# The mixer stage of a hybrid backbone layer in a fixed order of pieces per block, with the projection weights of the mixer in the tiles of the old activations

## The chip, the cores and the metric

One Trainium2 chip, one core of it. The metric is device time of one execution in microseconds (us), smaller is better. Engines are named as in the profile: PE (TensorE, matmuls), DVE (VectorE), ACT (ScalarE), POOL (GpSimd), SP (SyncE, which here only issues DMAs). One DMA queue is fed by SP, another by POOL.

## What is computed

One layer on 1024 tokens of width 1024, with 256 context tokens ahead of them, all in fp32. Cut to what matters here:

```python
u_x = rms_norm(x, norm1_w) * (1 + sc1) + sh1
pr_x = _prep(u_x, w_in, conv_w, conv_b, ...)   # projections; q and k of the mLSTM go through a 3x3 depthwise conv + SiLU
x_hg_f, x_hg_b = HGRN2 scans, forward and backward;  x_ml_f, x_ml_b = mLSTM scans, forward and backward
hg = head_rms_norm(x_hg_f + x_hg_b) * silu(pr['hg_g'])
ml = head_layer_norm(x_ml_f + x_ml_b) * sigmoid(pr['ml_o'])
x  = x + g1 * (concat([hg, ml]) @ w_out)                      # the mixer
v  = rms_norm(x, norm2_w) * (1 + sc2) + sh2
aff = softmax(v @ router_w)                                   # 16 experts
gate, idx = top_k(aff.T, 128)                                 # each expert chooses 128 tokens
x  = x + g2 * scatter_add(gate * swiglu_e(v[idx]))            # 16 experts, 3 weights of 1024 x 1024 each
out = rms_norm(x, final_norm_w)
```

## The kernel before, in words

The 1024 tokens are 8 blocks of 128. Products in fp32 are made of three matmuls of halves: an operand is split into a rounded part (`uh`, `wh`, `mh`: "hi") and what is left (`ul`, `wl`, `ml`: "lo"), and hi\*hi, hi\*lo and lo\*hi are summed.

The program runs in stages: context, modulation and the first projections (0 to about 205 us of the span); HGRN2 (to 465); the output gates, the convs and the backward states of the mLSTM (to about 690, the tuple `ORD` sets the order of these pieces); the **mixer stage** (to 916); the choice of the tokens (to 952); the experts (to the end). `uh` and `ul`, the split activations, are two tiles of 32 KB a partition that live until the last gate piece "o144" has run. After that `upool.close()` gives their room to the pool `mpb`, which holds the split of `w_out` (`woh`, `wol`, eight tiles each, L1107 to L1113).

In the mixer stage a loop over blocks `cc` (L1128) calls, in this order: `mixer(cc)` (48 matmuls of 128x512, in two halves of 24, L1027; the residual is added on DVE, L1028; stored to d_acc on POOL's queue, L1029); `scores(cc+3)` (loads `qk`, L935, and then `MB`, L936, the broadcast of the running maxima, 1024 pieces of 512 B; four matmuls L939; eight biased copies on ACT, L943; a minimum with the causal mask on DVE, L944; an add on POOL, L946; two Exp, L945 and L947; products on DVE); `mixed(cc+1)` (loads `kin` and `go`; four scalings on ACT, L1005; products on DVE or POOL; 8 transposes L1012; split into `mh` and `ml`); `outputs(cc+2)` (loads `sb`; updates the forward state; for each head four matmuls L975/L976 into a bank, then absolute value, maximum L978, reciprocal and two scaled copies that empty the bank) with `normed` (statistics and scaling); and for the block before, `router` (sum of squares, reciprocal root, v = x r A + B as one DVE operation L1052 and one POOL add L1053, stored on POOL's queue) and `logits`/`affinity` (8 transposes L1038, 8 matmuls L1042, softmax). So three blocks are in work at once, and a scheduler interleaves these calls on each engine by its own estimates. Behind block 5 the first four token blocks are sorted (16 rounds of maximum and replace, L760/L762, and merges), and behind block 6 two more; the last two behind block 7.

Around it, weights of the experts are fetched ahead into whatever buffers are free ("raws", L892), and two operands `qkx` and `MB` have two buffers each: `MB` of block c+2 can only be loaded when the `outputs` of block c has read its own. [...]

The conv (L820 to L830, eight times) computes nine taps: one by ACT into the sum, two by ACT with a POOL add each (L825), six by DVE (L827).

## Time and profile before

| | |
|---|---|
| median of 3 runs | 1564.99 us (1562.31 to 1569.66) |
| the profiled execution | 1563.71 us, its span 1561.6 us |
| PE busy | 1443.4 us (92%) |
| DVE busy | 1227.9 us (79%) |
| ACT busy | 873.6 us (56%) |
| POOL busy | 213.7 us (14%) |
| stores of the mixer's blocks 0, 4 and 7 to d_acc are issued at | 746.7, 854.1 and 916.3 us |

The profiled execution is 1.3 us under the median, and 2.1 us of it lie outside the span. PE is the engine with most work, and its idle time and the clock that it is granted say what a stage could save; idle time of the others costs nothing by itself. The profile's rows are times from the start of the span.

### The profile page before, as it was taken

What the parts mean: (1) busy time and instruction counts of PE and PEld (TensorE: products, weight loads), DVE (VectorE), ACT (ScalarE), POOL (GpSimd) and SP (SyncE); (2) the same over time, 40 slices, a digit from 0 to 9 for tenths busy, and PEclk for the clock granted to TensorE, in tenths of its full rate; (3) what the DMA queues carried; (4) which work ended last, traced back from release to release, by engine and by line L of the source; (5) the groups of instructions that cost most, each with busy time, mean ns of one, the idle gap of its engine ahead of it and who ended that gap; (6) DMA issues with size and microseconds to landing.
All of it is one profiled execution on the core that took longest, in us unless ns stands there. A gap on an engine that the chain in (4) does not pass through costs nothing.

```text
span 1561.6 us, 23094 instructions
## 1 busy us (share of the span) xinstructions
PE 1443.4 (92%) x8113; PEld 1207.2 (77%) x8113; DVE 1227.9 (79%) x2148; ACT 873.6 (56%) x1478; POOL 213.7 (14%) x165
## 2 busy tenths in 40 slices
...
PEclk9999999999999999988999977999999999999998
...
GB/s 253 263 136 31 109 54 35 75 82 15 122 102 142 82 149 138 118 175 219 200 140 120 155 329 226 369 390 370 384 391 383 388 389 383 382 385 356 343 148 108
DMA packets 181199, 337.29 MB, mean 216 GB/s; under 512 B 13560, under 2 KB 108348, under 8 KB 181084
## 3 DMA queue, kind: packets, MB, share of 16 engines
...
q8 instruction: 64, 1.05, 0.3%
q14 instruction: 51, 0.42, 0.1%
HBM read 303.38 MB, written 32.39 MB: 215 GB/s over the span
## 4 chain that ended last, share of the span: by engine, by line
PE 67%; DVE 12%; DMA 8%; issue 6%; ACT 4%; POOL 3%; ACTq 0%; SPq 0%; POOLq 0%; DVEq 0%
PE mm L1293 21%; PE mm L278 12%; PE hg L1293 11%; PE mm L286 8%; PE hg L350 3%; DMA MB<-d_nm 3%; PE ms L1278 2%; PE hg L215 2%; DMA d_go<-gsg 1%; PE ms L382 1%; DVE cacc L827 1%; DVE ac L297 1%; POOL MB L946 1%; PE hg L1383 1%; POOL wor L1073 1%
## 5 line engine op out<-in xcount | busy, mean ns | idle before, releaser
L286 PE MATMUL mm<-whi,uh 128*128 128x256 f32 (+1 forms) x512 | 145.8, 285 | 1.7 <-DVE utmp L198 0.9
L286 PE MATMUL mm<-wlo,uh 128*128 128x256 f32 (+1 forms) x512 | 145.1, 283 | 0.0
L286 PE MATMUL mm<-whi,ul 128*128 128x256 f32 (+1 forms) x512 | 144.7, 283 | 0.0
L253 DVE TENSOR_TENSOR wlo<-wraw,whi 128x512 fp32r<-128x512 f32 x96 | 65.5, 696 | 51.0 <-ACT whi L252 50.6
L286 PEld LDWEIGHTS mm<-whi,uh 128*128 128x128 f32 x512 | 96.6, 189 | 4.0 <-DVE utmp L198 1.1
L286 PEld LDWEIGHTS mm<-whi,ul 128*128 128x128 f32 x512 | 96.8, 189 | 0.0
L286 PEld LDWEIGHTS mm<-wlo,uh 128*128 128x128 f32 x512 | 96.4, 188 | 0.2
L1293 PE MATMUL mm<-qkx,xT 128*128 128x512 f32 x256 | 83.8, 408 | 0.7 <-ACT xT L1279 0.3
L1293 PE MATMUL mm<-E,xT 128*128 128x512 f32 x256 | 80.9, 397 | 0.4 <-ACT E L922 0.4
L1293 PE MATMUL mm<-MB,xT 128*128 128x512 f32 x256 | 80.3, 395 | 0.0
L252 ACT CAST whi<-wraw 128x512 fp32r<-128x512 f32 x96 | 58.3, 620 | 38.7 <-PE mm L278 24.8
L827 DVE SCALAR_TENSOR_TENSOR cacc<-pad,cols,cacc 128x1024 f32<-128x1024 f32 x48 | 65.3, 1360 | 17.9 <-POOL cacc L825 17.2
L344 ACT COPY hgc<-hgK 128x512 f32<-128x512 f32 x56 | 35.5, 634 | 78.1 <-DVE hgK L363 38.6
L350 PE MATMUL hg<-hgQ,hgc 128*128 128x128 f32 x448 | 65.9, 291 | 1.0 <-DVE hgQ L366 1.0
L350 PEld LDWEIGHTS hg<-hgQ,hgc 128*128 128x128 f32 x448 | 57.8, 191 | 10.8 <-issue 6.7
L278 PE MATMUL mm<-uh,whi 128*128 128x512 f32 x192 | 63.4, 405 | 0.0
L278 PE MATMUL mm<-ul,whi 128*128 128x512 f32 x192 | 63.3, 403 | 0.0
L1308 POOL DMA_INDIRECT vt<-d_v,idx x16 | 16.7, 1044 | 328.7 <-PE ms L1278 252.3
L297 DVE SCALAR_TENSOR_TENSOR ac<-wraw,csil,ac 128x256 f32<-128x256 f32 x112 | 58.2, 520 | 4.4 <-DMA wraw<-in_ada_w_dram 2.5
L278 PE MATMUL mm<-uh,wlo 128*128 128x512 f32 x192 | 61.5, 399 | 0.0
L1293 PEld LDWEIGHTS mm<-E,xT 128*128 128x128 f32 x256 | 47.5, 187 | 13.8 <-ACT E L922 2.2
L825 POOL TENSOR_TENSOR cacc<-cacc,cone 128x1024 f32<-128x1024 f32 x16 | 40.2, 2512 | 124.7 <-ACT cone L824 124.1
...
## 6 DMA issues: line engine op xcount, KB each, us to landing
...
```

Source lines behind the costliest of these rows:

```text
L215: T.matmul(pm[0:2, :256], csil[:, k, :], adas[i, k // 4][:, k % 4, :, :], start=(k == 0), stop=(k == 7))
L252: S.copy(hi[:, :, cs], src)
L253: V.tensor_sub(lo[:, :, cs], src, hi[:, :, cs])
L278: T.matmul(o, l, r[:, k, i * n:(i + 1) * n], start=(k == 0 and q == 0), stop=(k == 7 and q == 2))
L286: T.matmul(o, l[:, k, ts], r, start=(k == 0 and q == 0), stop=(k == 7 and q == 2))
L297: V.scalar_tensor_tensor(ac, a2[:, k % 4, :], csil[:, k, 0:1], ac, op0=OP.mult, op1=OP.add)
L344: S.copy(view(kc, 0, [[h, 2], [2 * h, 256 // h], [1, h]]), view(K, 0, [[512 + h, 2], [2 * h, 256 // h], [1, h]]))
L350: T.matmul(pb[:, cc, :], kc[:, cc * P:(cc + 1) * P], view(Q, cc * P, pat), start=True, stop=True)
L825: G.tensor_add(acc, acc, one)
L827: V.scalar_tensor_tensor(acc, tap(t), tapw(t, r), acc, op0=OP.mult, op1=OP.add)
L1278: T.transpose(pt[:, k, :], view(src, 4 * q + k, [[8, P]]), ident)
L1293: T.matmul(o, l[:, k, :], r[:, 512 * j:512 * j + 512], start=(k == 0 and p_ == 0), stop=(k == 7 and p_ == 2))
```

## The change

- `uh` and `ul` become sixteen tiles of two k-slices by 512 columns each (the pool `up` stays open, `at` finds a slice). The splits of `w_out` take over those tiles one by one (`split_wo`): the first four (k 0 to 3, tiles `uh0x`, `ul0x`) are split before the last gate piece "o144", the other four behind it.
- The conv's tap 1 goes from DVE to ACT with a third POOL add.
- The causal mask is now 0 or -1e30 and is added instead of a minimum taken: by DVE for blocks 0 to 2, by POOL for the others (`s_min`).
- The scaling of `hg` by its norm is one broadcast multiply (`m_hg`), on DVE for blocks 0 and 1 and on POOL for the others; it was four ACT operations.
- v = x r A + B is now one ACT multiply and a POOL multiply and add (`r_v`); the DVE operation L1052 is gone. The stores of d_acc and d_v go from POOL's queue to SP's.
- `MB` is loaded ahead of `qk` in `s_load`.
- The functions are cut into pieces, and the loop over blocks calls them in a fixed order under `tc.manual_schedule()`: each engine runs them as written.
- The first sort, 16 rounds, runs in single rounds that are strewn over blocks 4 to 6 (`rounds`); the second, of two token blocks, runs on 128 partitions by 64 values in 8 rounds (before: 64 by 128 in 16), its pairs of lists are merged by `lists`.
- The loop's first weights are still split early by the scheduler; `A2b`, `B2b` and `g1b` join the raw buffers as operands.

The core of the diff:

```diff
-    uh = up.tile([P, 8, 1024], F32R, name="uh")
-    ul = up.tile([P, 8, 1024], F32R, name="ul")
+
+    uh, ul = ([[up.tile([P, 2, 512], F32R, name=f"{n}{hf}{j}", tag=f"{n}{hf}{j}", bufs=1) for j in range(4)] for hf in range(2)] for n in ("uh", "ul"))
+
+    def at(u, k, a, b):
+
+        return u[a // 512][k // 2][:, k % 2, a % 512:(b - 1) % 512 + 1] if isinstance(u, list) else u[:, k, a:b]
...
-    V.tensor_scalar(cmask[:, 0, :], dd, 0.5, 1e30, op0=OP.add, op1=OP.mult)
-    V.tensor_scalar(cmask[:, 1, :], dd, -1.0, 0.5, op0=OP.mult, op1=OP.add)
-    V.tensor_scalar(cmask[:, 1, :], cmask[:, 1, :], 1e30, None, op0=OP.mult)
+    V.tensor_scalar(cmask[:, 0, :], dd, 0.0, -1e30, op0=OP.is_lt, op1=OP.mult)
+    V.tensor_scalar(cmask[:, 1, :], dd, 0.0, -1e30, op0=OP.is_gt, op1=OP.mult)
...
-        for t in (3, 5):
+        for t in (3, 5, 1):
             one = cvp.tile([P, 16, 64], F32, name="cone", tag="cone", bufs=2)
             S.mul(one, tap(t), tapw(t, r))
             G.tensor_add(acc, acc, one)
-        for t in (0, 1, 2, 6, 7, 8):
+        for t in (0, 2, 6, 7, 8):
...
+    st = {}
+
+    def s_load(cc):
+        qk, MB = st["qk", cc], st["MB", cc] = tl("qkx", [8, P], 2), tl("MB", [8, P], 2)
+        load(MB, bass.AP(tensor=d_nm.tensor, offset=d_nm.offset + cc * P, ap=[[0, P], [1024, 8], [1, P]]))
         load(qk, d_qk[cc])
...
+    def s_min(cc, eng=V):
+        E = st["E", cc]
+        for d in range(2):
+            eng.tensor_tensor(E[:, d], E[:, d], cmask[:, d, :].unsqueeze(1).to_broadcast([P, 4, P]), op=OP.add)
...
+    def m_hg(cc, eng):
+        hg, go = st["hg", cc], st["go", cc]
+        mix = st["mix", cc] = tb("mix", [8, P], 1)
+        eng.tensor_mul(hg, hg, hgr[:, cc, :].unsqueeze(2).to_broadcast([P, 4, P]))
+        eng.tensor_mul(mix[:, 0:4, :], hg, go[:, 0:4, :])
+
+    def m_ml(cc):
+        V.scalar_tensor_tensor(st["mix", cc][:, 4:8, :], st["go", cc][:, 4:8, :], 1.0, st["h", cc], op0=OP.add, op1=OP.mult)
...
+    def x_store(cc):
+        load(d_acc[cc * P:(cc + 1) * P], st["xm", cc])
...
+    def r_v(cc):
+
+        vt = st["vt", cc]
+        S.mul(vt, st["xm", cc], st["r2", cc])
+        G.tensor_mul(vt, vt, A2b)
         G.tensor_add(vt, vt, B2b)
-        kept["v"] = store(d_v[row], vt)
-        if dbg and "xm" in dbg:
-            nc.sync.dma_start(dbg["xm"][row], xm)
-            nc.sync.dma_start(dbg["v"][row], vt)
-        return r2
-
-    def affinity(cc, r2, pl):
+
+    def v_store(cc):
+        load(d_v[cc * P:(cc + 1) * P], st["vt", cc])
...
+    def split_wo(ks):
+
+        for k in ks:
+            for l, n in ((woh, "uh"), (wol, "ul")):
+                l.append(up.tile([P, 1024], F32R, name=f"{n}{k // 4}{k % 4}", tag=f"{n}{k // 4}{k % 4}", bufs=1))
+            S.mul(woh[k], wors[k], onw[:, k:k + 1])
+            V.scalar_tensor_tensor(wol[k], wors[k], onw[:, k:k + 1], woh[k], op0=OP.mult, op1=OP.subtract)
+            if k + 3 < 8:
+                load_wo(k + 3)
...
-           "o004", "k3", "u4", "o044", "k2", "u3", "k1", "u2", "o104", "M", "u1", "S0", "S1", "O0", "L0", "o144")
+           "o004", "k3", "u4", "o044", "k2", "u3", "k1", "u2", "o104", "M", "u1", "S0", "S1", "O0", "W", "o144")
...
+    x_load(0)
+    m_load(0)
+    m_load(1)
+    m_hg(0, V)
+    m_ml(0)
+    m_T(0)
+    split_wo(range(4, 8))
...
+    for f in (o_load, o_state, o_step, o_num, n_stat):
+        f(1)
+    for f in (s_load, s_mm, s_kT, s_sum, s_min, s_exp):
+        f(2)
+    o_load(2)
...
+    def sort_steps(dst, src, n, w=P):
+
+        buf = srw[len(sorts)]
+        sorts.append(dst)
+        for r in range(w // 8):
+            e8 = dst[:n, 8 * r:8 * r + 8]
+            V.max(e8, src[:n])
+            if r < w // 8 - 1:
+                V.match_replace(buf[:n, :w], e8, src[:n], -1.0)
+            src = buf[:, :w]
+            yield
...
+    with tc.manual_schedule():
+        for cc in range(8):
+            a, b, c, p = cc + 1, cc + 2, cc + 3, cc - 1
+            if c < 8:
+                s_load(c)
+                o_load(c)
+            if b < 8:
+                m_load(b)
+            if cc:
+                x_store(p)
+            mixer(cc, 0, range(4))
+            if cc:
+                l_T(p)
+            if a < 8:
+                n_norm(a)
+                m_ml(a)
+            if cc:
+                r_v(p)
+                v_store(p)
+            mixer(cc, 0, range(4, 8))
+            x_add(cc, 0)
+            if b < 8:
+                s_mul(b)
+            rounds(3)
+            if c < 8:
+                s_mm(c)
+                s_sum(c)
+                s_min(c, G)
+            mixer(cc, 1, range(3))
+            if c < 8:
+                s_kT(c)
+            if cc == 7:
+                l_mm(p)
+                a_exp(p)
+                best = merge(srt[:, 0, :], (64, 32), tmp)
+                a_div(p)
+            mixer(cc, 1, range(3, 5))
+            if a < 8:
+                m_T(a)
+            if b < 8:
+                m_hg(b, G)
+            rounds(3)
+            if 0 < cc < 7:
+                l_mm(p)
+                a_exp(p)
+                a_div(p)
+            if b < 8:
+                o_state(b)
+                o_step(b)
+            if c < 8:
+                s_exp(c)
+            mixer(cc, 1, range(5, 8))
+            if a < 8:
+                x_load(a)
+            if b < 8:
+                o_num(b)
+            x_add(cc, 1)
+            r_sq(cc)
+            if b < 8:
+                n_stat(b)
+            r_rs(cc)
+            if cc in (1, 3, 5):
+                old(cc // 2)
+                raw_load(1)
+            if cc == 4:
+                pt = bank("ms")
+                T.transpose(pt[:, :P], aff[:, 0].rearrange("p s e -> p (s e)"), ident)
+                S.copy(affS[:, 0, :], pt[:, :P])
+                sorting.append(sort_steps(srt[:, 0, :], affS[:, 0, :], P))
+            if cc in (5, 6):
+                rounds(2)
+            if cc == 6:
+                pt = affinities(0, 2)
+                for h in range(2):
+                    S.copy(srt[64 * h:64 * h + 64, 1, 64:P], pt[0:64, 64 * h:64 * h + 64])
+                sorting.append(sort_steps(srt[:, 1, 0:64], srt[:, 1, 64:P], P, 64))
+                r_ = lambda n, sh: tl(n, sh, 2, F32R)
+                sl = [part(r_("qkx", [8, P])) if i % 3 == 0 else part(r_("MB", [8, P])) if i % 3 == 1 else
+                      r_("E", [2, 4, P]).rearrange("p a b c -> p (a b c)") for i in range(6)]
+                sl += [flat3(mlp.tile([P, 2, 4, 129], F32R, name="v3", tag="v3", bufs=1)),
+                       flat3(const.tile([P, 2, 4, 129], F32R, name="mlc", tag="mlc", bufs=1))]
+                pairs.extend((sl[2 * i], sl[2 * i + 1]) for i in range(4))
+                early = []
+        x_store(7)
+        l_T(7)
+        rounds(8)
+        l_mm(7)
+        a_exp(7)
+        b2 = lists(srt[:, 1, :], tmp[0])
+        a_div(7)
+    b2 = merge(b2, (32,), [tmp[2]])
+    best = top(32, best[:32], b2[:32], tmp[0])
...
+    early += [split_w() for _ in range(4)]
```

**First place: SP's queue at the entry of the mixer stage.** The names: `go` is the gate of `mixed`/`m_load` (L1002 before, L1044 after), `wor` with `in_w_out_dram` a row block of `w_out` (L1072 before, L1136 after; with `in_exp_w_gate_dram` it is a raw weight of an expert, L894), `xm` the residual (L1021, L1067). Before:

```order
L1002 DMA go_6919<-d_go_58 128x1024
L1115 DMA xT_6974<-in_router_w_dram 128x128
L1117 DMA mods_6976<-d_g_64 128x2x8
L1072 DMA wor_6945<-in_w_out_dram 128x1024
L1072 DMA wor_6950<-in_w_out_dram 128x1024
L1021 DMA xm_7094<-in_x_dram 128x1024
L1072 DMA wor_6955<-in_w_out_dram 128x1024
L936 DMA MB_7150<-d_nm_63 128x8x128
```

And now:

```order
L938 DMA MB_7085<-d_nm_63 128x8x128
L1136 DMA wor_6823<-in_w_out_dram 128x1024
L984 DMA sb_7117<-d_sb_61 128x516
L1136 DMA wor_6830<-in_w_out_dram 128x1024
L1136 DMA wor_6837<-in_w_out_dram 128x1024
L1136 DMA wor_6990<-in_w_out_dram 128x1024
L894 DMA wor_7012<-in_exp_w_gate_dram 128x1024
L1067 DMA xm_6958<-in_x_dram 128x1024
L1044 DMA go_6961<-d_go_58 128x1024
```

The first `go`, which the first transposes of the mixer need, stood ahead of all `wor` loads but the first three; it now stands behind all eight of them and behind the first raw weight, whose buffer is a `wor` buffer.

**Second place: SP's queue in one block of the loop.** Block 3 before (some of it is for neighbouring blocks):

```order
L935 DMA qkx_8041<-d_qk_57 128x1024
L1001 DMA kin_8259<-d_hg_59 128x512
L936 DMA MB_7812<-d_nm_63 128x8x128
L1021 DMA xm_7756<-in_x_dram 128x1024
L959 DMA sb_8093<-d_sb_61 128x516
L1002 DMA go_8260<-d_go_58 128x1024
```

and block 3 now:

```order
L938 DMA MB_7784<-d_nm_63 128x8x128
L939 DMA qkx_7783<-d_qk_57 128x1024
L984 DMA sb_7787<-d_sb_61 128x516
L1043 DMA kin_7789<-d_hg_59 128x512
L1044 DMA go_7790<-d_go_58 128x1024
L1084 DMA d_acc_66<-xm_7490 128x1024
L1117 DMA d_v_65<-vt_7764 128x1024
L1067 DMA xm_7944<-in_x_dram 128x1024
```

`MB` was behind `qk` (the `qk` of its own block is some rows further up still), and is now ahead of it; the two stores have come in from POOL's queue.

**Third place: PE in one block, around the matmuls of the scores** (L939 before, L946 now; L1027 and L1077 are the mixer, L480/L482 and L1012/L1061 transposes). Before:

```order
L1027 MATMUL mm<-wl_6915,mh 128x512
L1027 MATMUL mm<-wh_6914,ml 128x512
L939 MATMUL hg<-qkx 128x128 x4
L480 MATMUL ms<-ident,qkx 128x128 x4
L1012 MATMUL ms<-ident,mix 128x128 x4
L496 MATMUL mm<-v_4837,mkt 128x129 x4
```

And now:

```order
L1077 MATMUL mm<-ul_7002,mh 128x512
L1077 MATMUL mm<-uh_7001,ml 128x512
L946 MATMUL hg<-qkx 128x128 x4
L1077 MATMUL mm<-uh_6812,mh 128x512
L1077 MATMUL mm<-ul_6813,mh 128x512
L1077 MATMUL mm<-uh_6812,ml 128x512
L1077 MATMUL mm<-uh_6819,mh 128x512
L1077 MATMUL mm<-ul_6820,mh 128x512
```

The scores' matmuls stood behind all 48 matmuls of the mixer's block; they now stand behind the first 24 of them, and the other 24 behind them.

## Rows read from the trace of the kernel before

**Rows 1.** The page's first row and the row of part 2 that gives the clock granted to PE in 40 equal slices of the span (tenths of full speed).
```profile
span 1561.6 us, 23094 instructions
PEclk9999999999999999988999977999999999999998
```
**Rows 2.** Five stretches: from and to, length, then for PE, PEld, DVE, ACT and POOL the busy time and in brackets the instructions, PE's mean granted clock, DMA share, GB/s.
```profile
722.00:747.00 25.00, 20.34 (x78) 15.40 (x78) 23.78 (x36) 15.72 (x32) 13.98 (x8) 0.78 0.77 278
747.00:771.00 24.00, 18.92 (x110) 15.83 (x109) 17.05 (x45) 14.25 (x42) 8.83 (x7) 0.99 0.54 186
825.50:854.00 28.50, 23.33 (x137) 20.65 (x138) 15.94 (x44) 14.40 (x40) 8.85 (x7) 0.94 0.50 131
854.00:916.30 62.30, 58.69 (x316) 49.97 (x317) 49.00 (x193) 21.75 (x56) 17.01 (x16) 0.92 0.52 177
952.00:1540.00 588.00, 582.71 (x2714) 468.50 (x2714) 551.93 (x603) 452.33 (x542) 45.80 (x36) 1.00 0.94 346
```
**Rows 3.** POOL's timeline: the issues of three of the eight stores of the residual (start, duration, in brackets the idle time before).
```profile
746.72 0.79 POOL L1029 DMA_DIRECT2D d_acc<-xm  x1 [2.06 <-DVE xm L1028]
...
854.07 0.60 POOL L1029 DMA_DIRECT2D d_acc<-xm  x1 [3.31 <-DVE xm L1028]
...
916.30 0.54 POOL L1029 DMA_DIRECT2D d_acc<-xm  x1 [10.27 <-DVE tkr L760]
```
**Rows 4.** What ACT waited for from 716 to 922: total us, times, longest.
```profile
ACT E L943 <- DMA MB<-d_nm: 17.0, 5, 5.7
```
**Rows 5.** PE's timeline at full clock (a duration includes the pipeline; the pitch is the distance of two starts).
```profile
784.17 0.39 PE L1027 MATMUL mm<-wl,mh 128*128 128x512 f32 x1
784.40 0.39 PE L1027 MATMUL mm<-wh,ml 128*128 128x512 f32 x1
...
790.75 1.06 PE L939 MATMUL hg<-qkx 128*128 128x128 f32 x8
791.65 0.60 PE L480 MATMUL ms<-ident,qkx 128*128 128x128 f32 x4
```
**Rows 6.** SP's timeline: the issues of three of the loads of `MB`, and of the one behind the second.
```profile
778.31 0.43 SPq L936 DMA_DIRECT2D MB<-d_nm  x1
...
805.75 0.37 SPq L936 DMA_DIRECT2D MB<-d_nm  x1
...
834.25 0.43 SPq L936 DMA_DIRECT2D MB<-d_nm  x1
```
**Rows 7.** ACT's timeline: the first operation on each of these three `MB`, in brackets how long ACT had waited for it.
```profile
790.25 2.45 ACT L943 ACTIVATE E<-MB,gT 128x128 f32<-128x128 f32 x8 [5.65 <-DMA MB<-d_nm]
815.70 0.40 ACT L943 ACTIVATE E<-MB,gT 128x128 f32<-128x128 f32 x1 [4.87 <-DMA MB<-d_nm]
...
845.83 2.45 ACT L943 ACTIVATE E<-MB,gT 128x128 f32<-128x128 f32 x8 [4.45 <-DMA MB<-d_nm]
```
**Rows 8.** The DMA view of 814.5 to 818.3 us, when what was issued behind that second `MB` came in.
```profile
DMA packets 517, 1.25 MB, mean 330 GB/s; under 512 B 53, under 2 KB 164, under 8 KB 517
```
**Rows 9.** PE's timeline at the entry of the mixer stage.
```profile
708.17 0.28 PE L286 MATMUL mm<-whi,ul 128*128 128x256 f32 x1
...
714.90 0.39 PE L976 MATMUL mm<-sb,MB 128*128 128x129 f32 x2
715.12 1.05 PE L939 MATMUL hg<-qkx 128*128 128x128 f32 x8
717.99 1.21 PE L1012 MATMUL ms<-ident,mix 128*128 128x128 f32 x8 [1.81 <-issue]
...
721.75 0.77 PE L1027 MATMUL mm<-wh,mh 128*128 128x512 f32 x1
```
**Rows 10.** SP's timeline there: the issue of the first `go`.
```profile
713.51 0.32 SPq L1002 DMA_DIRECT2D go<-d_go  x1
```
**Rows 11.** Groups of ACT's instructions from 716 to 922, shapes apart: count, busy us, mean ns, idle before.
```profile
L1050 ACT ACTIVATE vt<-xm 128x1024 f32<-128x1024 f32 x8 | 8.5, 1060 | 7.2 <-DVE xm L1028 5.9 <-issue 1.4
...
L1110 ACT ACTIVATE wh<-wor,cols 128x1024 fp32r<-128x1024 f32 x6 | 6.9, 1143 | 4.3 <-POOL wor L1073 4.3
```
**Rows 12.** The same for POOL, from 480 to 922.
```profile
L825 POOL TENSOR_TENSOR cacc<-cacc,cone 128x1024 f32<-128x1024 f32 x16 | 40.2, 2512 | 124.7 <-ACT cone L824 124.1
L1073 POOL TENSOR_TENSOR wor<-wor,g1b 128x1024 f32<-128x1024 f32 x8 | 19.7, 2474 | 35.2 <-DMA wor<-in_w_out_dram 22.5 <-DVE wl L1111 9.5 <-DVE bst L990 3.2
L1053 POOL TENSOR_TENSOR vt<-vt,B2b 128x1024 f32<-128x1024 f32 x8 | 18.9, 2367 | 9.7 <-DVE vt L1052 9.7
L946 POOL TENSOR_TENSOR MB<-MB,mu_b 128x1024 f32<-128x1024 f32 x8 | 18.7, 2341 | 56.7 <-ACT E L943 56.7
...
L1006 POOL TENSOR_TENSOR mix<-kin,go 128x512 f32<-128x512 f32 x5 | 7.7, 1534 | 3.0 <-PE ms L1012 1.5 <-ACT kin L1005 1.5
```
**Rows 13.** The same for DVE, from 716 to 922.
```profile
L978 DVE TENSOR_TENSOR den<-den,emn 128x2 f32<-128x2 f32 x27 | 17.4, 671 | 1.1 <-ACT den L977 1.1
L1052 DVE SCALAR_TENSOR_TENSOR vt<-xm,r,A2b 128x1024 f32<-128x1024 f32 x8 | 11.0, 1374 | 2.3 <-POOL r L155 2.3
L1111 DVE SCALAR_TENSOR_TENSOR wl<-wor,cols,wh 128x1024 fp32r<-128x1024 f32 x7 | 11.0, 1566 | 0.0
...
L944 DVE TENSOR_TENSOR E<-E,cmask 128x512 f32<-128x512 f32 x10 | 6.9, 688 | 12.7 <-ACT E L943 12.6
...
L979 DVE RECIPROCAL den<-den 128x2 f32<-128x2 f32 x27 | 3.2, 150 | 0.0
```
**Rows 14.** Groups of DVE's instructions from 480 to 690.
```profile
L827 DVE SCALAR_TENSOR_TENSOR cacc<-pad,cols,cacc 128x1024 f32<-128x1024 f32 x48 | 65.3, 1360 | 17.9 <-POOL cacc L825 17.2
```
**Rows 15.** PE's timeline behind the mixer: the last logits, and the wait for the chosen tokens.
```profile
918.05 3.60 PE L1042 MATMUL hg<-rwa,xT 128*128 128x16 f32 x16 [0.81 <-ACT xT L1039]
...
940.73 0.18 PE L1220 MATMUL ms<-cnt,low 128*128 128x3 bf16 x1 [16.85 <-DVE cnt L1218]
```

257 lines of the change are left out of this document (118 added, 139 removed).

## The prediction, made before the changed kernel ran

> **What bounds the kernel now.** Begin with the clock and the stretches. PE is granted full speed nearly everywhere; the reader is to see the slices that fall short, and that they lie where the mixer and the choice of tokens run [rows 1]. The stretches say what the mixer stage loses [rows 2]: in blocks 1 to 4 PE is busy 18.9 us of 24.0 and 23.3 of 28.5, so each block has about 5 us of idle PE, and the clock is 0.99 to 0.94 of full on top. In the experts PE is busy 582.7 of 588 us at full clock, so that stage moves as a whole: what is won or lost before it is kept.
>
> Next, the pace. The stores of blocks 0, 4 and 7 lie at 746.72, 854.07 and 916.30 [rows 3]: 107.35 us for blocks 1 to 4, 26.84 each, and 62.23 for blocks 5 to 7. What PE needs: a 128x512 matmul has a pitch of 0.23 us (784.17 to 784.40), eight small ones take 0.90 from 790.75 to 791.65, so 0.1125 each [rows 5]. A full block has 48 large and 84 small ones (8 transposes of the mix, 8 and 16 for the logits, 8 scores, 4 and 8 for the state, 32 for the outputs): 11.0 + 9.4 = 20.4 us. So 6.4 us of a block are not PE's work. What causes them is the load of `MB`: ACT waited for it five times, 17.0 us in all [rows 4], and behind ACT wait the minimum, two Exp, the products and the outputs, which free the buffer for the next `MB`. This loop sets the pace of blocks 1 to 4.
>
> **The change, part by part.**
>
> *Entry of the stage.* Before, the first `go` was issued at 713.51 [rows 10], its transposes ran at 717.99, the mixer from 721.75 [rows 9]. Now it is queued behind the last row block of `w_out` and a raw load that waits until all eight splits are done. The tiles for splits 4 to 7 come free when the last gate matmul has read them, 708.4 [rows 9]. Split 4 takes 1.14 on ACT [rows 11] and 1.57 on DVE [rows 13]: 711.1. Only then does the buffer for row block 7 come free: load about 3 us (the first `go` needed at most 4.5 from issue to its transposes), POOL's multiply 2.47 [rows 12], split 2.7: 719.3. Then raw, residual and `go`, each 512 KB at the 330 GB/s of [rows 8], 1.6 us apiece: 724. Product 0.7, transposes 0.9, copies 1.3: the mixer begins at about 727. That is **+5** (0, if the splits run ahead of the old schedule, to +8, if DVE's state steps come between). What it buys: block 0 no longer stalls on halves of `w_out` and starts with all weights there. Before, 722 to 747 went at 0.78 of the clock [rows 2]. PE will have idled before 727, so I leave some of the slow clock in: 20.4 + 3.4 + 0.2 = 24, **-1**.
>
> *Blocks 1 to 4.* The pieces now overlap: the `MB` of block c+3 is for the next block's outputs, so its chain through ACT, POOL and Exp has a block's time more. But `MB` is ahead of `qk` in SP's queue, and its buffer comes free only with the last matmul of the previous outputs, that is, at the block's start T. Issue to use was 11.94 (778.31 to 790.25), 9.95 and 11.58 us [rows 6, 7]; ACT waited in each, so these are landings. I take the shortest, 10.0, since the new order lets it start with less beside it. What was issued behind came in after it, at 330 GB/s [rows 8]: `qk` at T + 11.6. PE reaches the scores after 24 large matmuls and 8 transposes, T + 6.4. In order as PE is, it waits **5.2 us** in each of these blocks, with 24 mixer matmuls queued behind that could have run. A block becomes 20.4 + 5.2 = 25.6, and 0.8 for the clock (0.2 to 1.7 are lost in the two blocks of [rows 2]): 26.4 for 26.84, **-2** over four blocks. Ends: no wait, 21.2 a block, -23; a wait by the longest `MB` (7.1) with 1.7 for the clock, 29.2, +9.
> By the Trainium skill, "DMA: Bandwidth & Descriptors", section Specifications, a transfer moves at line rate from pieces of 512 B on, so `MB` should be no slower than `qk`. The rows here speak against that. By the rule no wait would be left, and the sum would be that of the first rival.
>
> *Cover in these blocks.* POOL gets the multiply of v (2.37 like the add L1053), two mask adds and the scaling of `hg` (1.53 each like L1006): per block 2 x 2.37 + 2.34 + 4 x 1.53 + 1.6 of roots = 14.8 us [rows 12], for 8.9 busy before [rows 2]. It fits in 26 us beside PE. DVE loses L1052 (1.37) and the minimum (2 x 0.69) [rows 13], ACT four scalings, and gains one multiply (1.06, as L1050 [rows 11]): off the path, at nothing. The two stores moved to SP stand ahead of the next residual there; they are due 20 us before it is used. If the cover is gone, that is the second rival.
>
> *Blocks 5 to 7.* No scores and no `MB` are left, so no wait on them. PE's work is 18.2 (48 large, 64 small), 14.6 (32 small) and 13.7 (24 small): 46.5. Before they took 62.23, with 58.69 counted busy at 0.92 of the clock [rows 2], and DVE busy 49.0 us of it. The strewn rounds take the long sort from there in part. DVE and the clock still cost something: I take 50.5, **-11.7** (46.5 to 56, so -16 to -6).
>
> *Behind the mixer.* The merges of the first list stand on DVE ahead of the last residual add, and `lists` ahead of the last softmax; against that the second sort has half the rounds. PE waited 16.85 for the choice, after logits at half clock [rows 15]. **+1** (-2 to +4).
>
> *Convs.* DVE loses 8 taps of 1.36 [rows 14], 10.9 us; POOL gets 8 adds of 2.51 [rows 12], and DVE's taps of each conv start that much later. PE leads there: **0** (-3 to +4). If the cover fails, the state steps behind a late conv on DVE are late next.
>
> Sum: 5 - 1 - 2 - 11.7 + 1 = -8.7, from 1563.71 to 1555.0; the median lies 1.3 above the profiled run: **1556**. A difference of 0.5% (7.8 us) is what can be told from no change here, so the forecast lies just beyond it.
>
> **Rivals.**
>
> *A: PE does not wait for `qk`.* For it: the three loads differ by 2 us, so what else is in flight matters, and with the stores in the same queue behind it `MB` may come sooner; the order keeps PE dense then, and the clock up. Against it: the shortest of three was still 9.95. Four blocks gain 5.2 and the clock's 0.8: 24 less, 1532.
>
> *B: POOL holds up DVE (the other side).* The tiny maximum L978, 128x2, took 671 ns on average where the reciprocal L979 of the same size took 150 [rows 13]: half a microsecond lost behind POOL at a POOL share of a third (8.8 of 24 and 8.9 of 28.5 [rows 2]). POOL's share now rises to 14.8 of 26, 57%, its operations are 1.5 to 2.4 us long, and four L978 stand in the chain that empties PE's banks at the block's end. If each hits a whole add (2.4), the outputs take up to 9 us longer; three free banks hide about half. Then a block costs 4 more: five blocks, +20: 1576. It decides from about 1.5 us per L978 on. For it: POOL's additions fall into each part of the block. Against it: PE already idles for `qk`, in which DVE catches up.
> The Trainium skill ("SBUF — State Buffer", section SBUF: two separate sides) has this as a lock of one port pair that the later of the two waits for; the 671 beside 150 agree.
>
> *C: the wait pulls the clock down.* Block 0 shows 0.78 [rows 2]; a single wait of over 5 us in each block, with the longer `MB`: 20.4 + 7.1 + 2.4 for the clock (between the 1.7 above and the 5.5 that 0.78 makes of 25 us) = 29.9, 3.5 more than 26.4 in each of four blocks: +14, 1570. Against it: 747 to 771 had 5.1 us of idle PE at 0.99.
>
> That the change does not do what it says is out: the pieces stand in the new order on every engine.
>
> **How the numbers follow.** The forecast has 0.42; its own bounds reach from 1548 to 1565, faster 0.24 of it and same 0.18. A has 0.25, faster. C 0.12: same 0.07, slower 0.05. B 0.21: slower 0.17, same 0.04. So faster 0.49, same 0.29, slower 0.22. The range, 1531 to 1576, takes in the points of A and C and reaches B's, and leaves out about the lower half of A and the upper half of B.
>
> **What would show it.** Mixer's first matmul near 727, not 722. In blocks 0 to 4 one wait of PE of about 5 us before L946, ended by the DMA of `qkx`, and mixer periods of 26 to 27; if it is absent and periods are near 21, A. L978 near 0.7 us; above 1.5, with PE waiting for banks in L1013, B. A granted clock under 0.9 in blocks 1 to 4, C. Blocks 5 to 7 in about 50 us. The forecast is wrong if the gain lies in blocks 1 to 4, if the last three are no faster, or if the convs or the choice of tokens move by over 5 us.

## The result: slower, 1.0116 of the kernel before

| kernel | median us | of executions | ratio to before, 95% interval |
|---|---|---|---|
| before | 1565.13 | 1561.37 to 1569.66 | 1 |
| changed | 1583.47 | 1577.27 to 1587.02 | 1.0116 [1.0089, 1.0143] |

The forecast was 1556, faster by half a percent; the kernel became slower by 1.2%, 18 us, beyond the upper end of the range. The profiled execution took 1587.02, the longest of its six, so the changed kernel was profiled a second time in the experiments (e16, span 1576.4). Where the two profiles differ, that is said below.

The page of the changed kernel: its first row, and the clock granted to PE in 40 slices. Against [rows 1] the clock's digits in the convolutions and the experts are the same; those of the mixer's slices changed.
```profile
span 1585.2 us, 23120 instructions
PEclk9999999999999999977989976999999999999998
```
Cut the stage where PE's first mixer matmuls of blocks 0, 1 and 5 start, where its last one ends, and where the first chosen tokens are gathered. These are the stretches of the kernel before (the columns are those of [rows 2]):
```profile
721.70:754.50 32.80, 25.60 (x118) 19.99 (x116) 30.96 (x55) 20.96 (x50) 15.61 (x10) 0.83 0.70 249
754.50:860.00 105.50, 88.85 (x493) 77.85 (x493) 60.66 (x168) 52.78 (x144) 36.86 (x29) 0.90 0.47 148
860.00:913.10 53.10, 50.33 (x262) 42.10 (x262) 40.43 (x162) 16.74 (x44) 14.09 (x13) 0.94 0.53 177
913.10:946.30 33.20, 9.11 (x63) 7.82 (x61) 28.11 (x151) 5.96 (x16) 4.10 (x5) 0.56 0.92 348
```
The same four of the changed kernel, first profile:
```profile
740.30:761.90 21.60, 20.86 (x115) 17.47 (x114) 11.15 (x27) 10.79 (x30) 7.85 (x6) 0.90 0.40 153
761.90:871.90 110.00, 91.89 (x528) 80.27 (x527) 59.08 (x162) 54.47 (x138) 54.68 (x36) 0.88 0.46 151
871.90:930.30 58.40, 50.67 (x267) 42.26 (x265) 40.29 (x137) 22.22 (x51) 21.89 (x13) 0.94 0.49 162
930.30:971.30 41.00, 7.26 (x38) 6.00 (x38) 32.35 (x165) 5.85 (x13) 5.23 (x3) 0.52 0.83 311
```
And its second profile:
```profile
734.60:755.40 20.80, 19.54 (x116) 16.30 (x115) 11.42 (x27) 10.79 (x30) 7.62 (x6) 0.97 0.48 158
755.40:863.00 107.60, 89.98 (x528) 78.61 (x526) 59.08 (x162) 54.50 (x138) 54.72 (x36) 0.92 0.46 155
863.00:921.30 58.30, 50.72 (x267) 42.29 (x265) 40.18 (x137) 22.21 (x51) 21.90 (x13) 0.94 0.49 163
921.30:962.40 41.10, 7.30 (x39) 6.01 (x38) 32.45 (x165) 5.84 (x13) 5.24 (x3) 0.53 0.83 310
```
Read the lengths. The mixer starts 18.5 us later in the first profile and 12.9 in the second, and block 0 is 11.2 and 12.0 shorter: in the second profile 0.9 of the late entry is left, in the first 7.4. Blocks 1 to 4 are longer by 4.5 and 2.1. **Blocks 5 to 7 are longer by 5.3 and 5.2, what lies behind the mixer by 7.8 and 7.9**, the same in both. From the first gather to the end it is 613.9 and 614.0, for 615.3 before. So the firm loss is 13 us from block 5 on, and PE's busy time in blocks 5 to 7 tells of what kind it is: 50.3 of 53.1 us before, 50.7 of 58.3 now. PE waits.

**The wait on `qk`, as forecast.** What PE waited for before the scores, 700 to 960 us of the first profile (total us, times, longest); then SP's two issues of one block and the scores in PE's timeline.
```profile
PE hg L946 <- DMA qkx<-d_qk: 18.6, 5, 4.7
```
```profile
762.13 0.38 SPq L938 DMA_DIRECT2D MB<-d_nm  x1
762.56 0.57 SPq L939 DMA_DIRECT2D qkx<-d_qk  x1
```
```profile
773.34 2.07 PE L946 MATMUL hg<-qkx 128*128 128x128 f32 x8 [4.74 <-DMA qkx<-d_qk]
```
`qk` was issued 0.43 us behind `MB` and used 10.8 us later; PE stood 4.74 us, where 5.2 had been worked out from [rows 6, 7]. `MB` itself had come in just before: ACT, which waited for it, began at 772.08, 9.95 us after the issue of `MB`. Eight score matmuls then took 2.07 us, about twice as long as [rows 5]: the clock was low there.

**The entry.** POOL's timeline, then DVE's two operations around its root and its first product with `go`, then ACT's and PE's (start, duration, in brackets the wait; first profile):
```profile
714.63 2.39 POOL L1137 TENSOR_TENSOR wor<-wor,g1b 128x1024 f32<-128x1024 f32 x1 [10.59 <-DMA wor<-in_w_out_dram]
716.98 1.47 POOL L158 TENSOR_TENSOR r<-r,mhalf 128x4 f32<-128x4 f32 x1
```
```profile
710.18 0.16 DVE L157 TENSOR_SCALAR r<-mv 128x4 f32<-128x4 f32 x1
...
718.48 1.86 DVE L1028 SCALAR_TENSOR_TENSOR nb<-mv,r 128x4 f32<-128x4 f32 x1 [0.91 <-POOL r L158]
...
737.75 0.69 DVE L1050 TENSOR_TENSOR mix<-kin,go 128x512 f32<-128x512 f32 x1 [0.78 <-DMA go<-d_go]
```
```profile
720.37 1.65 ACT L1035 ACTIVATE hsum<-hsum,nb,r 128x128 f32<-128x128 f32 x4 [4.18 <-DVE nb L1028]
721.92 0.36 ACT L714 ACTIVATE gsg<-mm 128x256 f32<-128x256 f32 x1
```
```profile
722.33 0.71 PE L498 MATMUL mm<-v,mkt 128*128 128x129 f32 x4 [2.86 <-ACT gsg L714]
...
740.30 0.79 PE L1077 MATMUL mm<-uh,mh 128*128 128x512 f32 x1
```
The root was ready to be taken at 710.3. POOL waited 10.59 us for a row block of `w_out`, multiplied it, and took the root at 716.98; the norm followed on ACT at 720.37, a gate stood behind it there, and PE waited for the gate. Later SP issued the first `go` at 730.58, behind all row blocks of `w_out`; DVE waited for it until 737.75, and the first transposes of the mixer came at 738.54. These delays are real. What they are worth is another matter (e2, e5, e11).

**Blocks 5 to 7 and behind.** PE's timeline in the second profile, waits alone, and below it DVE's around them:
```profile
887.15 0.80 PE L1013 MATMUL mm<-v,E 128*128 128x129 f32 x2 [5.16 <-DVE hsum L1019]
...
927.50 1.97 PE L1092 MATMUL ms<-ident,xm 128*128 128x128 f32 x8 [6.16 <-DVE xm L1081]
...
939.02 0.40 PE L796 MATMUL ms<-ident,tkr 128*64 128x128 f32 x1 [5.92 <-DVE tkr L1130]
...
956.31 0.19 PE L1380 MATMUL ms<-cnt,low 128*128 128x3 bf16 x1 [16.90 <-DVE cnt L1378]
```
```profile
877.83 0.28 DVE L1221 MAX8 tkr<-tkr 128x8 f32<-128x128 f32 x1
...
885.81 0.23 DVE L1130 TENSOR_SCALAR tkr<-tkr,sm 128x16 f32<-128x16 f32 x1
...
886.75 0.35 DVE L1019 SCALAR_TENSOR_TENSOR hsum<-mm,den,hsum 128x128 f32<-128x128 f32 x1 [0.44 <-ACT hsum L1018]
...
914.09 0.69 DVE L1081 TENSOR_TENSOR xm<-xm,mm 128x512 f32<-128x512 f32 x1 [3.93 <-PE mm L1077]
...
918.39 0.22 DVE L789 COPY S<-tkr 64x128 f32<-64x128 f32 x1
...
925.00 0.23 DVE L1130 TENSOR_SCALAR tkr<-tkr,sm 128x16 f32<-128x16 f32 x1
...
926.77 0.68 DVE L1081 TENSOR_TENSOR xm<-xm,mm 128x512 f32<-128x512 f32 x1
```
In block 5 six sort rounds and a softmax stand on DVE ahead of the outputs (877.83 to 886.0), and PE waits 5.16 us for a bank that the outputs must empty. In block 7 both merges run from 918.39 on (L789 begins the first), then a softmax (925.00) and three rounds of the second sort, all ahead of the last residual add: the last matmul ends at 921.3, the add starts at 926.77, and PE waits 6.16 us for it. Earlier DVE had stood idle (3.93 us at 914.09) with the merges queued behind. The choice, waited for until 940.73 in [rows 15], comes at 956.31: 35.0 us behind the last mixer matmul, against 27.6.

**GpSimd's new work.** Groups of DVE's instructions, 735 to 930 of the first profile; then an operation of POOL and the one of DVE that began within it:
```profile
L974 DVE TENSOR_TENSOR MB<-qkx,MB 128x512 f32<-128x512 f32 x12 | 24.6, 2052 | 0.0
...
L1016 DVE TENSOR_TENSOR den<-den,emn 128x2 f32<-128x2 f32 x26 | 3.9, 154 | 8.4 <-ACT den L1015 8.4
```
```profile
881.10 2.42 POOL L1113 TENSOR_TENSOR vt<-vt,A2b 128x1024 f32<-128x1024 f32 x1 [2.11 <-ACT vt L1112]
```
```profile
881.81 2.25 DVE L974 TENSOR_TENSOR MB<-qkx,MB 128x512 f32<-128x512 f32 x1
```
The tiny maximum, 671 ns in [rows 13], costs 154 now: from 730 us on none of them overlaps an operation of POOL. The product L974 has taken its place, 2.05 us on average. The one at 881.81 began while POOL multiplied (881.10 to 883.52) and ended 0.54 us behind POOL's end; two of the same kernel that ran while POOL was idle took 1.28 us together (699.42).

### The profile page after: what moved, and what is told of

The parts are those of the page before. It is cut to its first block, busy times and chain, and to the rows that moved or that the text cites. A ratio compares the mean times of both kernels' runs of the same rounds, so it can differ in the third digit from the quotient of the medians.

```text
span 1585.2 us, 23120 instructions
## 1 busy us (share of the span) xinstructions
PE 1449.1 (91%) x8113; PEld 1214.2 (77%) x8113; DVE 1210.7 (76%) x2112; ACT 882.1 (56%) x1463; POOL 262.0 (17%) x182
## 4 chain that ended last, share of the span: by engine, by line
PE 72%; DVE 10%; DMA 8%; issue 3%; ACT 3%; POOL 2%; SPq 0%; ACTq 0%; POOLq 0%; DVEq 0%
PE mm L1453 22%; PE mm L281 12%; PE hg L1453 10%; PE mm L288 8%; DMA qkx<-d_qk 3%; PE hg L352 3%; PE mm L1077 3%; PE ms L1438 2%; DVE cacc L829 2%; PE hg L218 2%; POOL cacc L827 1%; PE ms L384 1%; DMA MB<-d_nm 1%; DMA wor<-in_w_out_dram 1%; PE hg L1099 1%
## 5 line engine op out<-in xcount | busy, mean ns | idle before, releaser
L256 DVE TENSOR_TENSOR wlo<-wraw,whi 128x512 fp32r<-128x512 f32 x96 | 66.8, 709 | 50.9 <-ACT whi L255 50.3
L827 POOL TENSOR_TENSOR cacc<-cacc,cone 128x1024 f32<-128x1024 f32 x24 | 59.2, 2466 | 113.0 <-ACT cone L826 111.9
L829 DVE SCALAR_TENSOR_TENSOR cacc<-pad,cols,cacc 128x1024 f32<-128x1024 f32 x40 | 55.2, 1379 | 26.8 <-POOL cacc L827 26.4
L1468 POOL DMA_INDIRECT vt<-d_v,idx x16 | 16.2, 1014 | 333.1 <-PE ms L1438 252.7
L352 PEld LDWEIGHTS hg<-hgQ,hgc 128*128 128x128 f32 x448 | 57.8, 191 | 10.8 <-issue 6.7
L925 DVE TENSOR_TENSOR E<-uh,MB 128x1024 fp32r<-128x1024 f32 x48 | 58.7, 1223 | 6.5 <-ACT MB L924 6.5
L925 DVE TENSOR_TENSOR qkx<-ul,E 128x1024 fp32r<-128x1024 f32 x48 | 58.7, 1223 | 4.0 <-ACT E L924 3.7
```

The lines of the kernel that those rows point to most:

```text
L256: V.tensor_sub(lo[:, :, cs], src, hi[:, :, cs])
L352: T.matmul(pb[:, cc, :], kc[:, cc * P:(cc + 1) * P], view(Q, cc * P, pat), start=True, stop=True)
L827: G.tensor_add(acc, acc, one)
L829: V.scalar_tensor_tensor(acc, tap(t), tapw(t, r), acc, op0=OP.mult, op1=OP.add)
L925: V.tensor_sub(wl[:, cs], r, wh[:, cs])
```

## The experiments

Each kernel is compared with the kernel before on the same chip. "Ratio" is that comparison. First all of them, with the mixer's marks from PE's timeline (us, each to about 0.1; e16 is the changed kernel's second profile). The recorded expectations call `qk` the product rows, `MB` the mask rows and v = x r A + B the state's product.

| kernel | median | ratio, 95% interval | first mixer matmul | block 1 starts | blocks 1-4 | blocks 5-7 | to the first gather |
|---|---|---|---|---|---|---|---|
| before | 1565.13 | 1 | 721.7 | 754.5 | 105.5 | 53.1 | 33.2 |
| changed | 1583.47 | 1.0116 [1.0089, 1.0143] | 740.3 | 761.9 | 110.0 | 58.4 | 41.0 |
| e16 | 1579.21 | 1.0105 [1.0071, 1.0139] | 734.6 | 755.4 | 107.6 | 58.3 | 41.1 |
| e1 qk first | 1572.23 | 1.0063 [1.0039, 1.0086] | 739.1 | 759.7 | 96.7 | 58.4 | 41.1 |
| e2 splits late | 1583.80 | 1.0140 [1.0115, 1.0166] | 731.7 | 758.4 | 110.2 | 58.4 | 41.1 |
| e3 taps as before | 1575.30 | 1.0093 [1.0066, 1.0121] | 730.4 | 751.2 | 107.7 | 58.4 | 41.5 |
| e4 rounds moved | 1578.93 | 1.0110 [1.0084, 1.0137] | 732.6 | 753.4 | 108.0 | 58.8 | 41.4 |
| e5 entry | 1592.84 | 1.0188 [1.0166, 1.0209] | 737.1 | 770.6 | 109.1 | 58.4 | 41.1 |
| e6 = e1+e3+e5 | 1575.41 | 1.0084 [1.0061, 1.0106] | 730.6 | 763.2 | 95.0 | 58.4 | 41.1 |
| e7 end by scheduler | 1570.35 | 1.0051 [1.0031, 1.0072] | 733.6 | 754.5 | 109.9 | 55.2 | 33.5 |
| e8 GpSimd relieved | 1577.28 | 1.0097 [1.0073, 1.0121] | 731.5 | 752.6 | 109.5 | 58.7 | 39.0 |
| e9 = e1+e3+e7 | 1562.08 | 1.0003 [0.9988, 1.0019] | 735.6 | 756.5 | 100.2 | 55.2 | 33.5 |
| e10 = e9+e8 | 1557.71 | 0.9972 [0.9957, 0.9988] | 737.4 | 758.6 | 100.2 | 51.4 | 31.3 |
| e11 = e9+entry 2 | 1558.68 | 0.9982 [0.9967, 0.9998] | 729.4 | 755.6 | 101.2 | 55.0 | 33.5 |
| e12 all by scheduler, +e1+e3 | 1576.88 | 1.0103 [1.0070, 1.0135] | 731.3 | 755.6 | 112.4 | 54.9 | 32.8 |
| e13 sort free | 1573.63 | 1.0067 [1.0047, 1.0086] | 735.7 | 757.2 | 110.2 | 57.8 | 35.6 |
| e14 = e10+entry 2 | 1552.89 | 0.9935 [0.9915, 0.9956] | 728.0 | 754.0 | 100.6 | 51.5 | 31.1 |
| e15 = e14, sort free only | 1558.39 | 0.9969 [0.9952, 0.9985] | 725.7 | 751.8 | 98.2 | 55.8 | 33.6 |

**e1, the load order.**
```diff
-        load(MB, ...)
         load(qk, d_qk[cc])
+        load(MB, ...)
```


> The changed kernel with one edit: qk is loaded ahead of MB. Queue theory: PE's wait before the scores (18.6 us in five blocks, 4.6 each in the full ones) is qk standing in SP's queue behind the 1024 pieces of MB. Then the wait goes to under 1 us a block, PE's granted clock in blocks 1 to 4 rises from 0.88 to 0.93 or more, these blocks fall from 27.4 to about 21.5 to 23.5 us, and the kernel gains 15 to 24 us on the changed one: about 1560 to 1568, level with the kernel before. Rival (POOL holds DVE, and DVE empties PE's banks late): the time moves to a wait of PE for banks at the outputs, blocks stay over 26 us, the gain is under 6 us.

Two windows of four, blocks 1 and 4; SP's issues and the scores of block 2:
```profile
759.70:785.20 25.50, 23.99 (x135) 21.25 (x133) 14.98 (x41) 13.60 (x35) 13.69 (x9) 0.87 0.47 166
...
833.50:856.40 22.90, 21.00 (x131) 18.16 (x129) 14.86 (x40) 13.44 (x33) 13.71 (x9) 1.00 0.53 174
```
```profile
775.22 0.44 SPq L938 DMA_DIRECT2D qkx<-d_qk  x1
785.43 0.38 SPq L939 DMA_DIRECT2D MB<-d_nm  x1
```
```profile
791.82 1.05 PE L946 MATMUL hg<-qkx 128*128 128x128 f32 x8
```
The wait is gone, and the blocks take 96.7 us instead of 107.6 to 110. The clock is full in the last of them; over the four it is 0.93, where the changed kernel has 0.92 and 0.88. The kernel gains 0.5%, 7 to 11 us, less than the 15 to 24 expected: the blocks came to 24.2 us each and not to 21.5 to 23.5, and in three of them PE now waits for `mkt` from ACT, 5.0 us in all.

The edit changes two things at once. `qk` no longer stands behind the pieces of `MB`, and it no longer stands behind the wait of `MB` for a free buffer: it goes out 10.2 us ahead of `MB` in block 2, where in the changed kernel it went out 0.43 us behind it. The run does not separate the two. `MB` itself came no sooner: ACT, which waited for it, began at 795.73, 10.3 us after its issue.

**e2, the splits.** All eight stand behind the first transposes (the two halves of the tiles swapped, by when they come free).
```diff
...
         elif what == "W":
-            split_wo(range(4))
+            pass
...
     m_T(0)
-    split_wo(range(4, 8))
+    split_wo(range(8))
```


> The changed kernel, but all eight splits of w_out stand behind the first block's transposes, and the first four go into the tiles that the last gate piece frees (the halves of the tile names swapped), so no split and no load of w_out can run before that piece. POOL then has the root of block 0's norm ahead of the multiplies of w_out, as before the change, and go stands ahead of the last two loads of w_out on SP. Entry theory: the early splits made the entry late, by POOL waiting for a row block of w_out queued behind an MB, with the norm, the gates on ACT and so PE behind it, and by go queued behind all of w_out. Then the mixer's first matmul moves from 740 to 726 to 730, block 0 gives 1 to 4 us of it back in waits for splits, and the kernel gains 7 to 12 us on the changed one (about 1572 to 1577). Rival (the delay comes from the conv and the tiles' sixteen pieces ahead of it): the first matmul stays within 5 us of 740.

A miss. The first mixer matmul came at 731.7, but the block lasted 26.7 us, and block 1 started at 758.4, within what the changed kernel shows. ACT's and DVE's timelines show the new wait:
```profile
726.47 1.15 ACT L1146 ACTIVATE uh<-wor,cols 128x1024 fp32r<-128x1024 f32 x1 [2.13 <-POOL wor L1137]
```
```profile
727.97 1.26 DVE L1147 SCALAR_TENSOR_TENSOR ul<-wor,cols,uh 128x1024 fp32r<-128x1024 f32 x1
729.15 0.68 DVE L1050 TENSOR_TENSOR mix<-kin,go 128x512 f32<-128x512 f32 x1
```
The splits wait for POOL's multiplies, and the mix stands behind the splits on DVE. In block 0 PE then waits 3.4 us for `qk` and 1.3 us for an operand of the router. The entry as the cause of the loss fell here in its first form.

**e3, the taps.**
```diff
-        for t in (3, 5, 1):
+        for t in (3, 5):
...
-        for t in (0, 2, 6, 7, 8):
+        for t in (0, 1, 2, 6, 7, 8):
```


> The changed kernel with the conv's taps as before: two by ACT and POOL, six by DVE. Conv theory: PE is 5.0 us later against the kernel before between 515 and 673 us, in two steps of 2.4, because DVE's taps start one POOL add later and the state steps behind them on DVE hold PE's banks. Then both steps go and the gain on the changed kernel is 3 to 6 us (about 1578 to 1580), with PE's wait on the state step back from 5.7 to 4.4. Rival (the third add is hidden, the steps come from elsewhere in the order): gain under 2 us.

By the ratios 0.1 to 0.2% better than the changed kernel, inside their intervals; block 1 starts at 751.2, 4 us earlier than in e16, and PE's longest wait on the state step in the convs fell from 5.7 to 4.4 us, as the theory had it. The cost was put at 0 (-3 to +4); by the start of block 1 it is at the upper end of that.

**e4, the rounds within the hand order.** Block 5's rounds behind its outputs, the merge behind the last residual add.
```diff
-                best = merge(srt[:, 0, :], (64, 32), tmp)
...
-            rounds(3)
+            if cc != 5:
+                rounds(3)
...
-                rounds(2)
+                rounds(5 if cc == 5 else 2)
...
+        best = merge(srt[:, 0, :], (64, 32), tmp)
```


> The changed kernel with DVE's sorting moved behind what PE waits for: in block 5 the three rounds ahead of the outputs run at its end instead, and the merge of the first lists runs behind the last residual add instead of ahead of it. Order theory: DVE runs in the written order, so the 5.2 us wait of PE for a bank in block 5 (with about 3 us of clock behind it) and the last residual add, 5.4 us behind its matmuls, go; some of the merge is given back behind it, since the choice of the tokens then waits for it: gain 5 to 9 us (about 1574 to 1578). Rival (the choice at the end is DVE-bound, so sorting moved is sorting paid): gain under 2 us, with a longer wait of PE for the counts than 16.9.

No gain in the ratio, as the rival had it. PE no longer waits long for the last add (1.0 us at most), but the choice comes as late: blocks 5 to 7 and the way to the gather are 58.8 and 41.4. Moving the rounds later in the hand order pays one wait with the other.

**e5 and e6, the entry.** Row blocks 4 to 6 are loaded behind the first `go`, the first root stands ahead of their multiplies.
```diff
-            if k + 3 < 8:
+            if k + 3 in (3, 7):
...
+        m_load(0)
+        x_load(0)
+        for k in range(4, 7):
+            load_wo(k)
...
```


> The change with its entry rearranged: the early splits of row blocks 0 to 3 stay, but row blocks 4 to 6 of the output projection are loaded only after SP has released the first stores to be read back, and on GpSimd and ScalarE the first block's root and norm come ahead of the multiplies for row blocks 4 to 7. Theory: the entry is late (first mixer matmul 18.5 us later than before) because the loads and multiplies for these row blocks stand ahead of the first block's norm, masks and states on in-order queues; with that gone the first mixer matmul starts at 724 to 731 us instead of 740, and the run gains 9 to 15 us over the changed kernel: 1568 to 1574. Rival: VectorE waits for the late splits instead (row block 7 is loaded last) and the first block is stretched by as much as the entry gains, as happened when all splits stood late: 1579 to 1585, with block 0 at 26 us or more instead of 21.6.

> Three edits on the changed kernel together: the first product and norm rows loaded ahead of the block's mask rows, the convolution's taps divided among the engines as before, and the rearranged entry. Theory: the three causes lie in different stages and add: 11 (measured) + 5 to 8 (measured) + 9 to 15 (entry) off 1583, so 1549 to 1558, under the kernel before by 4 to 13 us. Rival: the entry only turns its wait into another, and the first two remain: 1563 to 1568, the same as before.

The rival held, with a worse size than it gave. POOL stood idle 20 us until the last row block was there in e5, and PE then waited 9.2 us for its split (8.6 in e6):
```profile
749.21 2.34 POOL L1137 TENSOR_TENSOR wor<-wor,g1b 128x1024 f32<-128x1024 f32 x1 [20.24 <-DMA wor<-in_w_out_dram]
```
Block 0 took 33 us in both. e6 against e5 shows that e1 and e3 stay worth what they were: 1.0% together, 0.8% by their ratios alone.

**e7, the end by the scheduler.** The same pieces; blocks 5 to 7 and the end have no fixed order.
```diff
-    with tc.manual_schedule():
-        for cc in range(8):
+    for cc in range(8):
+        with tc.manual_schedule() if cc < 5 else ExitStack():
...
```


> The changed kernel with the order written by hand for blocks 0 to 4 only; blocks 5 to 7 and the end are ordered by the scheduler from the same pieces. Theory: the missing 10 us of blocks 5 to 7 are lost to the waits on the first product rows and to the sort rounds, which the scheduler places no better: 1579 to 1587, no difference. Rival: the fixed order itself costs there (outputs and merges standing behind sort rounds on VectorE): then blocks 5 to 7 and what is behind them shorten by 6 to 10 us, 1573 to 1578.

The theory fell, and the rival held by more than it gave: 1570.35. Here is PE's wait for the last residual add, and DVE's first merge and that add:
```profile
922.40 1.97 PE L1092 MATMUL ms<-ident,xm 128*128 128x128 f32 x8 [2.82 <-DVE xm L1081]
```
```profile
895.46 0.22 DVE L789 COPY S<-tkr 64x128 f32<-64x128 f32 x1
...
921.68 0.67 DVE L1081 TENSOR_TENSOR xm<-xm,mm 128x512 f32<-128x512 f32 x1
```
The merges begin 26 us before the last residual add instead of 8 before it (895.46 to 921.68; 918.39 to 926.77 in the second profile). From block 5's start to the gather it is 88.7 us instead of 99.4 (from block 4's start 118.3 instead of 126.6; why the two differ is said at e13).

**e8, GpSimd relieved.** The mask, and the scaling and first product of v, on DVE.
```diff
-        S.mul(vt, st["xm", cc], st["r2", cc])
-        G.tensor_mul(vt, vt, A2b)
+        V.scalar_tensor_tensor(vt, st["xm", cc], st["r2", cc], A2b, ...)
...
-                s_min(c, G)
+                s_min(c)
```


> The changed kernel with the mask added by VectorE and the state's product formed by one VectorE operation in place of ScalarE's multiply and GpSimd's multiply; GpSimd keeps its other work. Theory: GpSimd's added work lies off the path, since TensorE's largest waits end with transfers; the run moves by no more than 3 us, 1580 to 1586. Rival: GpSimd's share of VectorE's memory port is what holds VectorE (its mask product takes 2.05 us instead of 0.74): then the blocks get 1 us or more shorter each, 1573 to 1578.

Alone it is unclear: the ratio is 0.1 to 0.2% below the changed kernel's, inside both intervals, and blocks 1 to 4 did not move.

**e9 to e12, together.** e9 is e1, e3 and e7; e10 adds e8; e11 adds to e9 a second entry, and e12 is e9 with `cc < 0` for `cc < 5`. The entry of e11:
```diff
         elif what == "W":
-            split_wo(range(4))
+            with tc.manual_schedule():
+                n_stat(0)
+                split_wo(range(3))
+                n_norm(0)
+                split_wo(range(3, 4))
...
-    x_load(0)
-    m_load(0)
-    m_load(1)
-    m_hg(0, V)
-    m_ml(0)
-    m_T(0)
-    split_wo(range(4, 8))
+    with tc.manual_schedule():
+        m_load(0)
+        split_wo(range(4, 5))
+        x_load(0)
...
+        split_wo(range(5, 8))
```


> Three repairs of the changed kernel together: the first product and norm rows loaded ahead of the block's mask rows, the convolution's taps divided as before, and the order written by hand for blocks 0 to 4 only. Theory: the causes lie in different places, so their gains add: 11 + 7 + 13 off 1583, less some 4 because the load order already helped in blocks 5 to 7, so 1553 to 1560, 4 to 11 us under the kernel before. Rival: the waits on the product rows in blocks 5 to 7 and the fixed order there are one and the same loss, so that only the larger counts: 1560 to 1566, the same as before.

> The same three repairs, and GpSimd's two added jobs (the mask and half of the state's product) given back to VectorE. Theory: GpSimd's share of the memory port lengthens VectorE's product by 1.3 us each and this was worth 6 us alone (1583 to 1577), so 3 to 6 us less than with three repairs. Rival: with the scheduler in blocks 5 to 7, where the gain of that edit lay, VectorE is the fuller engine and pays for the work it takes back: 0 to 4 us more than with three repairs.

> The same three repairs, and a second rearrangement of the entry: block 0's root and norm stand ahead of the fourth row block's multiply, row blocks 3 to 6 are loaded ahead of the first stores to be read back, and row block 7 right behind. Theory: ScalarE's gates no longer stand behind a norm that waits for GpSimd's multiplies; first mixer matmul 4 to 8 us earlier than with three repairs, and the run as much shorter. Rival: the late row block 7 makes the first mixer block wait, as in the first rearrangement: block 0 at 26 us or more and no gain, or a loss of up to 10 us.

> The changed kernel with the load order and the taps repaired and no order written by hand at all: the same pieces, ordered by the scheduler in all eight blocks. Theory: the hand order is worth its place in blocks 0 to 4, where its only large wait was the one on the product rows: against three repairs 5 to 15 us longer. Rival: the hand order costs there as it did in blocks 5 to 7: 3 us or more shorter than three repairs.

e9 is level with the kernel before. That lies in the rival's range, but the reason the rival gave is not what the ratios show: the three repairs gain 0.5, 0.2 and 0.65% alone by their ratios, 1.1% together, so most of it adds. e10 gains 4.4 us more, in blocks 5 to 7 and behind, as far as the theory had it. DVE's operation E (from v and MB, L925) there took 2.97 us in e9, where it began within an addition of POOL, and 1.19 in e10, where POOL was idle; POOL's busy time from block 5 on fell from 24.5 to 16.2 us. The scheduler also orders the pieces anew there, so it is not shown that all of the 4.4 us come from POOL. e11's first mixer matmul came 6 us earlier, but block 1 only 0.9 earlier: block 0 took 26.3 us, as the rival had it, and PE waited in it for ACT:
```profile
746.97 1.02 PE L1061 MATMUL ms<-ident,mix 128*128 128x128 f32 x4 [3.31 <-ACT mkt L486]
```
Its 3.4 us in the medians are not in these marks, and its interval overlaps that of e9. e12 is 14.8 us longer than e9, at the theory's upper end: by hand blocks 1 to 4 take 100.2, by the scheduler 112.4. So the hand order is good in blocks 1 to 4 and bad from block 5 on.

**e13 to e16, what in the hand order costs.** e13 keeps the hand order in all blocks, but the 16 rounds of the first sort and the merges are issued ahead of block 5 outside of it, and the scheduler weaves them in. e14 joins what helped; e15 is e14 with e13's order.
```diff
+        if cc == 5:
+            rounds(16)
+            best = merge(srt[:, 0, :], (64, 32), tmp)
+        with tc.manual_schedule():
...
```


> The changed kernel with the order written by hand in all eight blocks, but the first sort's 16 rounds and its two merges left to the scheduler, which weaves them between the other VectorE work of blocks 5 and 6 instead of three at a time. Theory: the rationing is what costs; the merges end before block 7, last mixer matmul to first gather falls from 41 us to 33 to 35, and the run gains 7 to 12 us over the changed kernel: 1571 to 1576. Rival: the hand order of the other pieces costs (outputs of block 7 and the mix behind the mixer's halves): a gain of at most 3 us, 1580 to 1585.

> Four repairs and the second entry together: product rows ahead of the mask rows, taps as before, order by hand for blocks 0 to 4 only, GpSimd's two added jobs back on VectorE, and the entry with block 0's root ahead of the fourth multiply. Theory: the last two were worth 4.4 and 3.4 us against three repairs and lie in different stages, so 1553 to 1556, 0.4 to 0.6% under the kernel before. Rival: with VectorE doing the mask and the product, the entry's splits meet a fuller VectorE and the entry's gain is gone: 1557 to 1559.

> The same as four repairs and second entry, but with the order by hand in all eight blocks and only the first sort with its merges left to the scheduler. Theory (the rationed sort was the cost, the hand order of the other pieces is good): as fast as with the scheduler in blocks 5 to 7, or up to 4 us faster: 1550 to 1556. Rival (the hand order of the other pieces costs): 4 to 9 us slower than that kernel, 1558 to 1564.

> The changed kernel itself, profiled again. Theory: part of the late entry belongs to the one execution that was profiled; the first mixer matmul comes at 731 to 735 us instead of 740, as in the kernels that share its code up to there, and the stretch from block 5's start to the first gather stays at 97 to 101 us. Rival: the entry is late in every execution, 738 to 742.

Half and half. e13 came out at 1573.63, which the theory's range holds, but on the same chip the changed kernel (e16) took 1579.21, so the gain is 5.6 us, between theory and rival: from block 5 to the gather 93.4 us, where e16 has 99.4 and e7 88.7. PE's waits in e13:
```profile
889.51 0.49 PE L1013 MATMUL mm<-v,E 128*128 128x129 f32 x2 [3.13 <-DVE hsum L1019]
...
926.17 1.16 PE L1092 MATMUL ms<-ident,xm 128*128 128x128 f32 x8 [1.01 <-DVE xm L1081]
...
937.41 0.39 PE L796 MATMUL ms<-ident,tkr 128*64 128x128 f32 x1 [7.58 <-DVE tkr L1130]
```
The wait for the last add has shrunk from 6.16 to 1.01; that for the last softmax has not (5.92, now 7.58). e15 against e14 says the same with the other repairs in, for the rival: with only the sort free it is 5.5 us slower, 89.4 us from block 5 to the gather against 82.6. e16 confirmed its theory: the first mixer matmul at 734.6.

One caution on these stretches. In e7 block 4 is 29.6 us long, 2.5 more than in e16, since the scheduler puts some of DVE's work of block 5 and a wait of 1.6 us ahead of PE's first matmul of block 5; the mark itself has moved. From block 4's start, which lies ahead of all that these runs change, it is 126.6 us to the gather in e16, 120.4 in e13 and 118.3 in e7; 113.0 in e15 and 108.4 in e14. So the free sort is worth 6.2 us, and the scheduler's order of the other pieces 2.1 more in e7 and 4.6 in e14. Between e13 and e7 the intervals of the ratios overlap.

**e14 is the fastest: 1552.89, ratio 0.9935 [0.9915, 0.9956]**, against 1.0116 for the change, at the lower end of what its theory gave. Its blocks 5 to 7 and the way to the gather:
```profile
854.60:906.10 51.50, 50.61 (x265) 42.59 (x265) 46.25 (x185) 18.36 (x47) 13.30 (x9) 0.93 0.55 192
906.10:937.20 31.10, 6.42 (x38) 5.32 (x38) 24.70 (x117) 4.61 (x12) 2.89 (x2) 0.56 0.94 363
```
In blocks 5 to 7 PE is now busy 50.6 us of 51.5.

## Why the prediction was wrong

**Entry and block 0: the sum held, not its parts.** Forecast +5 and -1. The mixer's start moved by +12.9 to +18.5, and block 0, start to start, by -12.0 to -11.2: +0.9 in the second profile, +7.4 in the first. The queue that was meant to be late (the last row block, raw, `go` on SP) was late: `go`, in by 724 in the forecast, was used at 737.75 and 732.00. Two things came on top that the forecast had not seen: the last gate matmul, taken at 708.4, ended at 719.0 and 714.1, and POOL's root stood behind the fourth multiply. But e2 and e11 brought the first matmul forward and block 1 hardly: it starts at 751 to 762 in every kernel but e5 and e6, which loaded the last row block late. A late first matmul is not a late block 1, since an earlier start met other waits in block 0: for `qk` in e2 (3.4 us), for ACT in e11 (3.3 us). Of the changed kernels only e5 and e6 waited for halves of `w_out`. That +5 and -1 added up to near the measured sums is luck.

**Blocks 1 to 4: the mechanism held.** The wait was 4.3 to 4.7 us for 5.2. Change forecast -2, measured +2.1 and +4.5: the term for the clock was too small. It stood at 0.8 us a block; granted clocks of 0.92 and 0.88 over 90 and 92 us of busy PE are 7 to 11 us in the four, about 2 to 3 a block. The trace of before had that price: its own four blocks stand at 0.90, and the two stretches of [rows 2] that the term came from, 0.99 and 0.94, were among the better ones. Between the marks there are also 35 more of PE's instructions than before (528 for 493), 3.9 us at the 0.1125 of the forecast, which the kernel before ran outside these blocks. Rival C, a clock pulled down by the wait, is not borne out: 0.92 and 0.88 lie on both sides of the 0.90 of before, and e1, without the wait, has 0.93. e1 shows what the wait and all that hangs on it are worth: 11 to 13 us in four blocks. Rival A, no wait, had four blocks 24 us shorter than the forecast's by its sum; without the wait they came out 11 to 13 us shorter, at 24.2 us each, with the clock still at 0.93 and a new wait for ACT.
The Trainium skill ("DMA: Bandwidth & Descriptors", section Specifications) would have had `MB` at line rate with its pieces of 512 B; `MB`, used 9.95 us after its issue in the changed kernel and 10.3 us in e1, speaks against it once more.

**Blocks 5 to 7: the step that failed.** Forecast 50.5 us, -11.7. Two faults. The first is the base: the 62.23 of [rows 3] run from the store of block 4 to that of block 7, and 5.9 us of them lie ahead of block 5's first matmul (854.07 to 860.0). By the mixer's own starts only 53.1 were there to save from, with PE busy 50.3 of them. Even by the forecast's own marks the gain stayed away: the stores of blocks 4 and 7 lie 61.2 us apart in both profiles (875.21 to 936.41, 866.30 to 927.48), for 62.2 before. The second fault is the reason given: "the strewn rounds take the long sort from there in part". They do the opposite. A fixed order holds a round back until its place comes, though DVE is idle, and holds back what is behind the rounds, though PE waits for it. Shown: freeing the first sort alone is worth 6.0 us from block 5 to the gather (99.4 to 93.4; 5.6 in the medians), and freeing the other pieces too brings it to 88.7, of which 2.1 are a gain and the rest a moved mark (4.6 with the other repairs in, e15 against e14). The kernel before has 86.3.

**Behind the mixer: right sign, wrong size.** Forecast +1 (-2 to +4), measured +7.9. The merges ahead of the last add were named; what they would cost there was not worked out: 918.39 to 925.00 alone is 6.6 us, and PE waited 6.16.

**Rival B, the other side, had the right sign for another reason.** Its place was wrong (L978, now L1016, is free of it) and its point of decision, 1.5 us, was passed by L974 instead, off the path in blocks 1 to 4. Taking the work off POOL is worth 4.4 us, in blocks 5 to 7, once the order there is repaired (e10); alone it is not resolved (e8). The Trainium skill ("SBUF — State Buffer", section SBUF: two separate sides) has a shared port behind such delays, locked for a whole instruction by the engine that starts first; that L974 at 881.81 ended 0.54 us behind POOL's operation, and that E took 2.97 us within one and 1.19 without, agrees with it.

**Convs: 0 held** within the bounds given, at their upper end (e3).

In sum, by the second profile: +0.9, +2.1, +13.1 from block 5 on, -1.3 behind the gather, 14.8 us in the spans; the forecast had +4, -2, -10.7 and 0.

Open: why block 1 starts no earlier than 751 whatever the entry; whether e11's 3.4 us over e9 are real, of which block 1's start accounts for 0.9; which of the two things that e1 changes took the wait away; and which of the other pieces in the hand order of blocks 5 to 7 costs the 2 to 5 us. An order by hand with the last softmax ahead of the second sort's rounds was not tried.
